# Both MLP up projections: the first four pairs' weights and pair 0's sums are made among the rows of the projection before, and the transposed quarters are asked for earlier

## The chip, the cores and the metric

One core of a Trainium2 chip runs the whole kernel. The metric is the time of one execution in microseconds (us) on the device; the kernel before takes 2149.13 us, the median of three runs (2148.42 to 2152.03).

The engines are called as in the profile: PE (TensorE, matmuls and transposes), DVE (VectorE), ACT (ScalarE), POOL (GpSimd) and SP (SyncE, which here only issues loads). Each runs its own queue of instructions in order, and semaphores tie the queues together.

## The reference, cut to what matters

A trunk of two layers runs over a sequence of 1024 rows and 1024 columns, all in float32. Each layer has a mixer (a gated short convolution in layer 0, latent attention in layer 1), whose output is projected, normed, gated and added to the stream, and then an MLP:

```
D_MODEL, SEQ, DEPTH, D_FF = 1024, 1024, 2, 4096

def squared_relu_mlp(h, w_up, w_down):
    return jnp.square(jax.nn.relu(h @ w_up)) @ w_down

# in each layer; y is the mixer's output (conv_out or attn_o projection)
x = x + g_m[:, None, :] * rmsnorm(y, norm_g[l, 1])
h = modulate(rmsnorm(x, norm_g[l, 2]), sh_f, sc_f)
y = squared_relu_mlp(h, mlp_up_w[l], mlp_down_w[l])
x = x + g_f[:, None, :] * rmsnorm(y, norm_g[l, 3])
```

The change touches the passage from the first of these lines to the start of `h @ w_up`. It comes twice: after conv_out in layer 0 (338 to 470 us of the profiled execution) and after attn_o in layer 1 (1457 to 1590 us).

## The kernel before, in words

**A product.** Every float32 operand is split into a high and a low part, and `mm` (L154 to L156) forms a product from three matmuls of 128x128 by 128x512. `split_w` (L158 to L160) makes the parts: ACT copies the high one (L159), DVE subtracts it for the low one (L160).

**The rows.** The projection ahead of the MLP (`down`) works in chunks of its contraction; in the last two chunks each of the eight tiles of 128 rows is one result `big` of two banks. In the middle chunk DVE adds it to the row's tile `y` (L870). In the last chunk a class `Seam` takes each row: DVE adds the result (L866) and multiplies by the gate (L328), ACT squares and sums (L271, L273), DVE forms the reciprocal (L278) and adds to the stream (L361), ACT squares again, and `flush` (L311) writes the normed row. The second half of row t is put down one row later, so that engines overlap. From row 5 on, `front` also transposes finished rows (PE, L409; ACT evacuates them with scale and shift, L410) and `back` splits the results (DVE, L420 and L421) one row later.

**The up projection** takes the columns of w_up in 16 pairs of two tiles of 128. A pair is a 2x2 block product by Winograd's scheme: 7 products instead of 8, each 4 steps of k by 3 matmuls, 84 matmuls in all. The right operands are made once: "11" and "21" from the first 512 rows (k tiles 0 to 7, `front0` and `back0`), and "22", "t1", "t2", "t3", "t4" from both halves in four quarters (`front1`, `back1`): in each quarter ACT evacuates two transposes, DVE makes four differences (L441, L443, L446, L448) and four low parts (L434) plus one more, nine DVE instructions in all, and ACT makes five high parts (L431). The left operands of a pair are made by `pair_sums`: DVE adds and subtracts blocks of two weight tiles (L510, L511, L515, L518), and the sums are split (t2, s2 and t3: names `uplo`, `s`). The tiles of one pair's products are `first` ("11"), then "21", t2 with s2 (key 6), t3 with "t3" (key 7), t2 with "t1" (5), t3 with "22" (3) and t2 with "t4" (4).

**The first pairs.** `first_pairs` bridges the time until the second half of the rows is normed. The pairs 0 to 3 need only "11" and "21" for their first two products, so these are run first, out of three weight tiles that were split ahead of the last chunk, and a fourth (`late`, name `w`) that comes in a buffer of its own. Pair 0's other five products are then run quarter by quarter as the quarters appear (`for kk in range(4)`). The order on PE, DVE and ACT is pinned there as it is written. Pairs 1 to 15 run in `all_pairs`: product 6, product 7, product 5, then 3 and 4, with `take` (L564) between 6 and 5 and between 5 and 3, since these three share one bank. The outputs of a pair are squared on ACT (L1150 to L1154), summed on DVE (L1161 to L1164) and stored by DMAs that ACT issues (L1166). A scheduler sets the order on each engine outside the pinned parts.

**Buffers.** `raw` tiles (512 KB) have four buffers for everything: weights, stream rows and the quarters' transposes. The split weights (`uphi`, `uplo`) have three each. The quarters' sums share one buffer (`gmb`).

## Time and profile before

| what | value |
|---|---|
| median of three runs | 2149.13 us (2148.42 to 2152.03) |
| the profiled execution | 2148.73 us, its span 2146.9 us |
| PE busy | 2057.8 us, 96% |
| DVE busy | 1542.4 us, 72% |
| ACT busy | 1085.8 us, 51% |
| mean granted TensorE clock | 0.992 |
| PE waits on other engines, 330 to 480 us | 10.4 us in 8 waits |
| the same in layer 1, 1455 to 1600 us | 10.6 us |

The span runs from the first to the last instruction, and 1.8 us of the profiled execution lie around it. A row of a timeline gives the start and the duration of an instruction (or of a few alike), then the engine, the line, what is written and read, and in square brackets the idle time before it with the engine and tile that ended it. A row of the waits gives the waiting instruction, what it waited for, the sum, the count and the longest. In the windows, PEclk is the clock that TensorE was granted, 1.00 being full speed.

### The profile page before, as it was taken

To read this page: it belongs to the slowest core of one execution; us is meant where nothing else is said; L and a number is where in the kernel's file an instruction comes from. 1 tells how busy PE (TensorE), PEld (TensorE's weight loads), DVE (VectorE), ACT (ScalarE), POOL (GpSimd) and SP (SyncE) were. 2 spreads that over 40 slices of the span, in tenths; PEclk is the share of its full clock that TensorE was granted. 3 is DMA by queue.
4 is the path that set the end of the run, shared out by engine and by line. 5 is a ranking of instruction groups with operands and counts; after the bars stand their busy time and mean duration, and the time that the engine had idled before them with its cause. 6 is when DMAs were issued, how large, how long until landed. Compare 5 with 4: busy or idle time off the path is not lost.

```text
span 2146.9 us, 25090 instructions
## 1 busy us (share of the span) xinstructions
PE 2057.8 (96%) x9438; PEld 1685.5 (79%) x9438; DVE 1542.4 (72%) x2100; ACT 1085.8 (51%) x1545; POOL 5.3 (0%) x13
## 2 busy tenths in 40 slices
PE   4999999899999999999899999999899999999998
PEld 3788878778888788888677788878678888788886
DVE  6877876875765669977688887757875665566577
ACT  4533354744554444455665565555644444544443
POOL 0000000000000000000000000000000000000000
PEclk9999999999999999999999999999999999999999
DMA  7444464254653889656223331144254653774255
GB/s 226 118 140 147 137 201 143 89 181 162 196 182 127 288 280 324 210 172 201 79 70 120 94 91 35 60 130 147 89 183 148 211 182 135 266 251 161 94 174 174
DMA packets 251167, 344.47 MB, mean 160 GB/s; under 512 B 19269, under 2 KB 142498, under 8 KB 251046
## 3 DMA queue, kind: packets, MB, share of 16 engines
q1 hardware_dynamic: 208840, 253.81, 37.7%
q10 hardware_dynamic: 42206, 89.06, 11.1%
q8 instruction: 74, 1.21, 0.2%
q14 instruction: 47, 0.39, 0.1%
HBM read 258.94 MB, written 83.89 MB: 160 GB/s over the span
## 4 chain that ended last, share of the span: by engine, by line
PE 74%; DVE 12%; ACT 6%; DMA 5%; issue 2%; SPq 0%; ACTq 0%; DVEq 0%
PE one L156 39%; PE mm L156 19%; PE tp L156 6%; PE big L156 5%; PE big L1397 2%; DMA raw<-ha 2%; DVE ring L160 1%; PE tp L1423 1%; ACT junk L271 1%; ACT slot L1247 1%; DMA w<-in_mlp_down_w_dram 1%; ACT ring L159 1%; DMA aw<-in_ada_w_dram 1%; DVE acc L186 1%; DVE uplo L160 1%
## 5 line engine op out<-in xcount | busy, mean ns | idle before, releaser
L156 PE MATMUL one<-slot,uphi 128*128 128x512 f32 x1224 | 377.9, 390 | 0.0
L156 PEld LDWEIGHTS one<-slot,uphi 128*128 128x128 f32 x1224 | 230.4, 188 | 48.2 <-issue 0.5
L156 PE MATMUL one<-ring,ring 128*128 128x512 f32 x1152 | 262.9, 389 | 2.3 <-DVE ring L160 2.3
L160 DVE TENSOR_TENSOR uplo<-raw,uphi 128x1024 fp32r<-128x1024 f32 x127 | 153.2, 1222 | 146.2 <-ACT uphi L159 146.2
L156 PEld LDWEIGHTS one<-ring,ring 128*128 128x128 f32 x1152 | 215.8, 188 | 48.3 <-ACT ring L159 3.1
L156 PE MATMUL one<-slot,uplo 128*128 128x512 f32 x612 | 240.7, 393 | 8.2 <-DVE y L564 3.8
L160 DVE TENSOR_TENSOR ring<-raw,ring 128x1024 fp32r<-128x1024 f32 x144 | 174.3, 1219 | 55.1 <-ACT ring L159 54.7
L159 ACT ACTIVATE ring<-raw 128x1024 fp32r<-128x1024 f32 x144 | 149.4, 1051 | 116.0 <-DMA raw<-ha 73.5
L159 ACT ACTIVATE uphi<-raw 128x1024 fp32r<-128x1024 f32 x127 | 134.6, 1061 | 122.0 <-PE one L156 80.2
L156 PE MATMUL mm<-ring,ring 128*128 128x512 f32 x768 | 185.0, 390 | 1.1 <-DVE ring L160 1.0
L156 PE MATMUL tp<-ring,ring 128*128 128x512 f32 x768 | 184.0, 389 | 0.0
L156 PEld LDWEIGHTS mm<-ring,ring 128*128 128x128 f32 x768 | 143.7, 188 | 31.7 <-DVE ring L160 1.4
L156 PEld LDWEIGHTS tp<-ring,ring 128*128 128x128 f32 x768 | 144.1, 188 | 29.9
L159 ACT ACTIVATE ring<-w 128x1024 fp32r<-128x1024 f32 x80 | 84.6, 1058 | 160.2 <-PE tp L156 86.6
L160 DVE TENSOR_TENSOR ring<-w,ring 128x1024 fp32r<-128x1024 f32 x80 | 97.7, 1221 | 77.5 <-ACT ring L159 76.8
L156 PEld LDWEIGHTS one<-slot,uplo 128*128 128x128 f32 x612 | 115.2, 188 | 35.9 <-DVE y L564 5.5
L186 DVE SCALAR_TENSOR_TENSOR acc<-raw,csil,acc 128x1024 f32<-128x1024 f32 x88 | 112.4, 1277 | 23.1 <-DMA raw<-in_ada_w_dram 18.3
L562 ACT ACTIVATE y<-one 128x512 f32<-128x512 f32 x66 | 39.0, 591 | 160.4 <-PE one L156 113.8
L156 PE MATMUL mm<-slot,uphi 128*128 128x512 f32 x344 | 107.4, 394 | 9.3 <-DVE slot L434 9.3
L156 PE MATMUL one<-slot,s 128*128 128x512 f32 x468 | 112.9, 390 | 1.1 <-DVE s L160 1.1
L156 PEld LDWEIGHTS one<-slot,s 128*128 128x128 f32 x468 | 87.6, 188 | 20.6 <-DVE s L160 2.4
L156 PE MATMUL one<-q,uphi 128*128 128x512 f32 x328 | 101.9, 392 | 0.0
(273 smaller groups left out, 3611.6 us busy)
## 6 DMA issues: line engine op xcount, KB each, us to landing
ha<-y ACTq DMA_DIRECT2D x224, 256.0 KB, 4.0
raw<-ha SPq DMA_DIRECT2D x112, 512.0 KB, 4.1
raw<-in_ada_w_dram SPq DMA_DIRECT2D x80, 512.0 KB, 4.2
raw<-in_mlp_up_w_dram SPq DMA_DIRECT2D x70, 512.0 KB, 4.5
w<-in_mlp_down_w_dram SPq DMA_DIRECT2D x48, 512.0 KB, 7.2
raw<-in_mlp_down_w_dram SPq DMA_DIRECT2D x32, 512.0 KB, 4.2
xs<-raw ACTq DMA_DIRECT2D x19, 512.0 KB, 3.1
raw<-in_conv_in_w_dram SPq DMA_DIRECT2D x18, 512.0 KB, 4.0
```

Of the source, the lines that this page charges most:

```text
L156: nc.tensor.matmul(out_, lhs[a], rhs[b], start=first and i == 0, stop=last and i == 2, skip_group_check=more)
L159: nc.scalar.activation(hi, src, AF.Copy)
L160: nc.vector.tensor_tensor(lo, src, hi.bitcast(F32), op=ALU.subtract)
L186: nc.vector.scalar_tensor_tensor(acc, raw, s, acc, op0=ALU.mult, op1=ALU.add)
L271: nc.scalar.activation(junk[:, :src.shape[-1]], src, AF.Square, accum_out=ss)
L562: nc.scalar.activation(dst, x_, AF.Copy)
L1247: nc.scalar.activation(y[32 * i:32 * i + 32, :], p_[32 * j:32 * j + 32, :], AF.Copy, scale=scale)
L1397: nc.tensor.matmul(o_, a, m_, start=j == 0, stop=j == 4)
L1423: nc.tensor.transpose(p_[:, c:c + P], pts[4 * hf + i][:, j * P:(j + 1) * P], ident)
```

## The change

In neutral words, and with the lines of the kernel after in brackets where they are meant:

1. The `ahead` step before the last chunk now splits four weight tiles instead of three, loads pair 0's two weight tiles and makes pair 0's sums and two of its three splits. `uphi` and `uplo` have five buffers each while the up stage lasts. The fourth weight tile takes a `raw` buffer; the buffer `late` is gone. The six loads stand on SP ahead of the rows' loads; three of them (two of pair 0, and `w`) stood behind them.
2. `Seam.tile` issues the transposes before the squares and the flush of the row, from row 5 on.
3. `first_pairs` runs first(0) and first(1) back to back, the four last "11"/"21" transposes behind them, and asks for each quarter's transposes one quarter earlier (`middle`, called in the midst of `back1`). The evacuations (`keep`, `gate`) are separate steps. Pair 0's products run in the order 3, 7, 5, 6, 4 in each quarter, 7 later in the last. t3's split stands behind quarter 0.
4. Pair 1's weights are loaded in `first_pairs`, and its sums are made there, behind the last quarter, by `pair_sums_apart`, which writes one difference into another tile. The last four of pair 0's additions (`finish`) and its store are handed to `all_pairs` and run in pair 1. Pair 1's result of product 7 goes to an `mm` bank.

The number of instructions of each engine is the same before and after, and so is what is computed. PE's order differs only in the passages named; DVE's, ACT's and SP's also differ through the rest of the up stage, since the scheduler has two more buffers of split weights there.

Three places in the order of DVE carry the prediction; all are in layer 0, and layer 1 has the like. First, the last rows of the middle chunk, before (L870 is a row's addition, L866 the last chunk's row 0):

```order
L160 TENSOR_TENSOR uplo_2605<-raw_2602,uphi_2604 128x1024
L870 TENSOR_TENSOR y_2272<-y_2272,big_2502 128x1024
L870 TENSOR_TENSOR y_2273<-y_2273,big_2516 128x1024
L870 TENSOR_TENSOR y_2274<-y_2274,big_2530 128x1024
L870 TENSOR_TENSOR y_2275<-y_2275,big_2544 128x1024
L866 TENSOR_TENSOR y_2268<-y_2268,big_2608 128x1024
```

and after, where L932 and L928 are the same additions, L525 to L533 pair 0's sums, and `uplo` and `s` the low parts of the splits:

```order
L172 TENSOR_TENSOR uplo_2611<-raw_2608,uphi_2610 128x1024
L525 TENSOR_TENSOR raw_2614<-raw_2614,raw_2616 128x512
L932 TENSOR_TENSOR y_2273<-y_2273,big_2516 128x1024
L526 TENSOR_TENSOR raw_2616<-raw_2616 128x512
L932 TENSOR_TENSOR y_2274<-y_2274,big_2530 128x1024
L172 TENSOR_TENSOR uplo_2621<-raw_2616,uphi_2620 128x1024
L530 TENSOR_TENSOR raw_2616<-raw_2616,raw_2614 128x512
L932 TENSOR_TENSOR y_2275<-y_2275,big_2544 128x1024
L172 TENSOR_TENSOR s_439_2626<-raw_2616,s_438_2625 128x512
L533 TENSOR_TENSOR raw_2614<-raw_2614,raw_2616 128x512
L928 TENSOR_TENSOR y_2268<-y_2268,big_2630 128x1024
```

Six instructions of pair 0 and the fourth weight's low part (`uplo_2611`) now stand between the rows' additions. Second, what stands ahead of the first quarter's first difference (L441), before:

```order
L420 CAST slot_2261<-q_2282 128x512
L421 TENSOR_TENSOR slot_2261<-q_2282,slot_2261 128x512
L278 RECIPROCAL small_3089<-small_3022 128x1
L160 TENSOR_TENSOR uplo_3106<-w_3041,uphi_3105 128x1024
L510 TENSOR_TENSOR raw_3043<-raw_3043,raw_3045 128x512
L511 TENSOR_TENSOR raw_3045<-raw_3045 128x512
L160 TENSOR_TENSOR uplo_3125<-raw_3045,uphi_3124 128x1024
L515 TENSOR_TENSOR raw_3045<-raw_3045,raw_3043 128x512
L160 TENSOR_TENSOR s_547_3143<-raw_3045,s_546_3142 128x512
L518 TENSOR_TENSOR raw_3043<-raw_3043,raw_3045 128x512
L441 TENSOR_TENSOR sums_3173<-raw_3128 128x512
```

and after (L453 is that difference):

```order
L432 CAST slot_2261<-q_2280 128x512
L433 TENSOR_TENSOR slot_2261<-q_2280,slot_2261 128x512
L290 RECIPROCAL small_3083<-small_3044 128x1
L432 CAST slot_2261<-q_2281 128x512
L433 TENSOR_TENSOR slot_2261<-q_2281,slot_2261 128x512
L432 CAST slot_2261<-q_2282 128x512
L433 TENSOR_TENSOR slot_2261<-q_2282,slot_2261 128x512
L453 TENSOR_TENSOR sums_3145<-raw_3118 128x512
```

The weight and the sums are gone from there, and the reciprocal (L278, now L290) on which the last row's flush waits stands four instructions earlier. Third, from the second `take` of pair 1 (L564) to the low part of pair 2's s2 (`s_592`), before:

```order
L564 TENSOR_TENSOR y_3403<-y_3038,one_3386 128x512
L1162 TENSOR_TENSOR y_3037<-y_3037,y_3371 128x512
L575 TENSOR_TENSOR y_3403<-y_3403,one_3430 128x512
L1163 TENSOR_TENSOR y_3417<-y_3037 128x512
L160 TENSOR_TENSOR uplo_3465<-raw_3459,uphi_3464 128x1024
L1164 TENSOR_TENSOR y_3418<-y_3371,y_3417 128x512
L515 TENSOR_TENSOR raw_3459<-raw_3459,raw_3457 128x512
L584 TENSOR_TENSOR y_3038<-y_3038,one_3386 128x512
L518 TENSOR_TENSOR raw_3457<-raw_3457,raw_3459 128x512
L160 TENSOR_TENSOR s_592_3470<-raw_3459,s_591_3469 128x512
```

and after, from the second instruction behind that `take` (now L604) on, L526 of pair 2 being the first:

```order
L615 TENSOR_TENSOR y_3346<-y_3346,mm_3430 128x512
L525 TENSOR_TENSOR raw_3562<-raw_3562,raw_3564 128x512
L526 TENSOR_TENSOR raw_3564<-raw_3564 128x512
L1234 TENSOR_TENSOR y_3098<-y_3098,y_3345 128x512
L172 TENSOR_TENSOR uplo_3465<-raw_3459,uphi_3464 128x1024
L1235 TENSOR_TENSOR y_3417<-y_3098 128x512
L530 TENSOR_TENSOR raw_3459<-raw_3459,raw_3457 128x512
L1236 TENSOR_TENSOR y_3418<-y_3345,y_3417 128x512
L533 TENSOR_TENSOR raw_3457<-raw_3457,raw_3459 128x512
L624 TENSOR_TENSOR y_3100<-y_3100,one_3395 128x512
L630 TENSOR_TENSOR y_3346<-y_3346,mm_3430 128x512
L172 TENSOR_TENSOR s_592_3470<-raw_3459,s_591_3469 128x512
```

Between the `take` and `s_592` stand now twelve instructions where there were eight: L525 and L526 of pair 3, L526 of pair 2 and L630, pair 1's last addition, have come into this stretch.

The diff, with the code that left `first_pairs` cut (it is printed above):

```
@@ -340,13 +352,13 @@
                     gained(slice(0, HALF if part else D))
                 else:
                     self.back()
+                if t >= 5:
+                    self.front(steps, 2)
                 if part:
                     ss = squares(self.nx, y[:, :HALF], some)
                 else:
                     ss = squares(self.nx, y)
                 self.flush()
-                if t >= 5:
-                    self.front(steps, 2)
                 rs = rroot(ss)
                 if not beside:
                     nc.vector.scalar_tensor_tensor(y, y, rs, self.gmb, op0=ALU.mult, op1=ALU.mult)
@@ -443,6 +455,7 @@
             part1("t1", kk, a)
             part2("22", kk, b)
+            middle()
             nc.vector.tensor_tensor(b, b, a, op=ALU.subtract)
             part1("t2", kk, b)
@@ -478,6 +491,8 @@
+    up_bufs = [3]
@@ -490,8 +505,8 @@
     def up_split(up, r3, kk=KD):
-        hi = up.tile([P, KD, P], F32R, tag="uphi", name=nm("uphi"), bufs=3)
-        lo = up.tile([P, KD, P], F32R, tag="uplo", name=nm("uplo"), bufs=3)
+        hi = up.tile([P, KD, P], F32R, tag="uphi", name=nm("uphi"), bufs=up_bufs[0])
+        lo = up.tile([P, KD, P], F32R, tag="uplo", name=nm("uplo"), bufs=up_bufs[0])
@@ -520,6 +535,22 @@
         t3 = up_split(up, a)
         yield {7: (t3, 0, "t3"), 3: (t3, 4, "22")}
+    def pair_sums_apart(up, a, b, s_):
+        a11, a12, a21, a22 = a[:, 0:4, :], a[:, 4:8, :], b[:, 0:4, :], b[:, 4:8, :]
+        s_ = s_.rearrange("p (k m) -> p k m", k=4)
+        nc.vector.tensor_tensor(a11, a11, a21, op=ALU.subtract)
+        nc.vector.tensor_tensor(s_, a22, a11, op=ALU.subtract)
+        s2 = tuple(up.tile([P, 4, P], F32R, tag="s2" + "hl"[i], name=nm("s2"), bufs=1) for i in range(2))
+        nc.scalar.activation(s2[0], s_, AF.Copy)
+        nc.vector.tensor_tensor(a21, a21, a22, op=ALU.add)
+        nc.vector.tensor_tensor(a12, a12, s_, op=ALU.subtract)
+        nc.vector.tensor_tensor(s2[1], s_, s2[0].bitcast(F32), op=ALU.subtract)
+        t3 = up_split(up, a)
+        yield {6: (s2, 0, "t2"), 7: (t3, 0, "t3"), 3: (t3, 4, "22")}
+        t2 = up_split(up, b)
+        yield {5: (t2, 0, "t1"), 4: (t2, 4, "t4")}
@@ -528,15 +559,18 @@
-    def all_pairs(up, ops, jobs):
...
-        end = []
+    def all_pairs(up, ops, jobs, end=()):
...
+        end, mark = list(end), None
         for raws, begun, quarter, done, between in jobs:
-            ra, rb = raws()
+            begun, *made = begun if isinstance(begun, tuple) else (begun,)
+            mark, mark_ = last_dve() if made else None, mark
+            if not made:
+                ra, rb = raws()
@@ -551,10 +585,16 @@
-            rest = {}
-            for part in pair_sums(up, ra, rb):
-                rest.update(part or {})
-            b = row_tile()
+            if made:
+                b, rest = made
+            else:
+                rest = {}
+                sums_ = pair_sums(up, ra, rb)
+                with behind(mark_):
+                    next(sums_)
+                for part in sums_:
+                    rest.update(part or {})
+                b = row_tile()
@@ -568,7 +608,7 @@
-            v = bank_ps()
+            v = mm_ps() if made else bank_ps()
             prod(v, rest[7], ops)
@@ -622,64 +662,86 @@
             seam.back()
         return ps_
...
+    def first_pairs(seam, steps0, steps1, up, wmat, ws, ops, pair):
         banks(True)
         tiles = [mm_ps(), mm_ps(), bank_ps(), bank_ps()]
...
+        ca = []
+        sums, rest = pair
         def first(i):
             prod(tiles[i], (ws[i], 0, "11"), ops)
+        def keep(i):
+            ca.append(row_tile())
             nc.scalar.activation(ca[i][:, HALF:], tiles[i], AF.Copy)
         def second(i):
             prod(tiles[i], (ws[i], 4, "21"), ops, False)
+        def gate(i):
             nc.scalar.activation(ca[i][:, :HALF], tiles[i], AF.Relu)
...
+        def front():
+            seam.front(steps1, 1)
+        def quarter(middle=lambda: None):
+            seam.backs.pop(0)(middle)
+        out_ = {}
+        def rest_of(kk, order):
+            for j in order:
+                prod(out_[j], rest[j], ops, kks=[kk])
         with pinned():
             first(0)
+            first(1)
+            seam.flush()
+            seam.front(steps0, 2)
+            keep(0)
+            keep(1)
+            first(2)
             seam.back()
...
+            front()
+            keep(2)
             second(0)
...
+            quarter(front)
+            gate(0)
+            rest.update(next(sums))
             second(1)
...
+            gate(1)
+            quarter(front)
             second(2)
...
+            gate(2)
             first(3)
...
+            keep(3)
+            out_.update({6: mm_ps(), 5: mm_ps(), 3: bank_ps(), 7: bank_ps(), 4: bank_ps()})
+            rest_of(0, (3, 7, 5, 6, 4))
+            quarter(front)
+            a, b = load_pair(wmat, 1)
+            second(3)
+            gate(3)
+            rest_of(1, (3, 7, 5, 6, 4))
+            quarter()
+            cb, b1 = row_tile(), row_tile()
+            rest_of(2, (3, 7, 5, 6, 4))
+            rest_of(3, (3, 5, 6, 7, 4))
+            sums = pair_sums_apart(up, a, b, b1[:, :HALF])
+            rest1 = next(sums)
+            p1 = ca[0][:, HALF:]
             c21, c22 = halves(cb)
             nc.vector.tensor_tensor(c21, p1, out_[6], op=ALU.add)
             nc.vector.tensor_tensor(c22, c21, out_[5], op=ALU.add)
+            rest1.update(next(sums))
+        def finish():
             nc.vector.tensor_tensor(c21, c21, out_[4], op=ALU.add)
             nc.vector.tensor_tensor(p1, c22, out_[3], op=ALU.add)
             nc.vector.tensor_tensor(c22, c22, out_[7], op=ALU.add)
             nc.vector.tensor_tensor(c21, c21, out_[7], op=ALU.add)
...
+        return ca, cb, (b1, rest1), finish
     def release_arena():
         for q in (ar[2], ar[1], ar[0]):
@@ -1132,13 +1194,23 @@
         steps0, steps1 = quarter_steps(ys, key, hs)
-        wcols = [next_w[:, 2 * i * P:(2 * i + 1) * P] for i in range(AHEAD - 1)]
-        down(slots, sizes, wd, src_fn, ys, seam, steps0, 0, lambda: ws.extend(up_weights(up, [w]) for w in wcols), begun)
-        return up, hs, first_pairs(seam, steps0, steps1, up, next_w, ws, hs)
+        wcols = [next_w[:, 2 * i * P:(2 * i + 1) * P] for i in range(AHEAD)]
+        up_bufs[0] = AHEAD + 1
+        pair = []
+        def ahead():
+            ws.extend(up_weights(up, [w]) for w in wcols)
+            sums = pair_sums(up, *load_pair(next_w, 0))
+            next(sums)
+            next(sums)
+            pair.extend([sums, next(sums)])
+        down(slots, sizes, wd, src_fn, ys, seam, steps0, 0, ahead, begun)
+        return up, hs, first_pairs(seam, steps0, steps1, up, next_w, ws, hs, pair)
     def mlp_up(l, up, ops, firsts, per_pair_bg):
-        ca, cb = firsts
+        ca, cb, made, finish = firsts
         late = []
         n = D_FF // P // 2
@@ -1174,14 +1246,16 @@
-        store(0, ca[0], cb)
-        end = all_pairs(up, ops, [(lambda i=i: load_pair(mlp_up_w[l], i), ca[i] if i < AHEAD else None, quarter,
-                                   lambda a, b, i=i: store(i, a, b), lambda i=i: between(i)) for i in range(1, n)])
+        begun = [None, (ca[1], *made), *ca[2:]] + [None] * (n - AHEAD)
+        end = all_pairs(up, ops, [(lambda i=i: load_pair(mlp_up_w[l], i), begun[i], quarter,
+                                   lambda a, b, i=i: store(i, a, b), lambda i=i: between(i)) for i in range(1, n)],
+                        [lambda: store(0, ca[0], cb), finish])
...
         up.release()
+        up_bufs[0] = 3
```

More of the change, by code (lines that the diff above doesn't have):

```diff
@@ L111, in pinned, with last_dve, behind @@
             last[ins.engine] = ins.name
+    def last_dve():
+        return [ins.name for ins in nc.cur_bb.bb.instructions if ins.engine == mybir.EngineType.DVE][-1]
+    @contextmanager
+    def behind(name):
+        n = len(nc.cur_bb.bb.instructions)
+        yield
+        if name:
+            ins = next(i for i in nc.cur_bb.bb.instructions[n:] if i.engine == mybir.EngineType.DVE)
+            tc.add_manual_dep(ins, name, NO_SYNC, reason="behind")
     def ld(out_, in_):
@@ L644, in first_pairs @@
             seam.back()
-            seam.front(steps0, 2)
-            first(1)
-            seam.back()
-            seam.flush()
+            front()
+            keep(2)
             second(0)
-            ws.append(up_split(up, late))
-            sums = pair_sums(up, a, b)
-            next(sums)
+            quarter(front)
+            gate(0)
+            rest.update(next(sums))
             second(1)
-            next(sums)
-            seam.front(steps1, 1)
-            rest = next(sums)
@@ L657, in first_pairs @@
-            first(2)
-            seam.front(steps1, 1)
-            seam.backs.pop(0)()
+            gate(1)
+            quarter(front)
             second(2)
-            rest.update(next(sums))
+            gate(2)
             first(3)
-            seam.front(steps1, 1)
-            seam.backs.pop(0)()
-            out_ = {6: mm_ps(), 5: mm_ps(), 3: bank_ps(), 7: bank_ps(), 4: bank_ps()}
-            for kk in range(4):
-                for j in (5, 6, 4, 3, 7):
-                    prod(out_[j], rest[j], ops, kks=[kk])
-                if kk == 0:
-                    second(3)
-                    seam.front(steps1, 1)
-                if kk < 2:
-                    seam.backs.pop(0)()
```

11 lines of the change are left out of this document (2 added, 9 removed).

## The prediction

> **What bounds the kernel now.** I read the page's busy times first, then PE's waits by stage, and last the timelines of PE, DVE and ACT in the stage that the change touches.
>
> ```profile
> PE 2057.8 (96%) x9438; PEld 1685.5 (79%) x9438; DVE 1542.4 (72%) x2100; ACT 1085.8 (51%) x1545; POOL 5.3 (0%) x13
> ```
>
> PE is busy for 96% of the span, so a change that adds and removes no work can only give back PE's waits, or make new ones. Here are PE's waits on other engines between 330 and 480 us, all of layer 0's passage:
>
> ```profile
> PE mm L156 <- DVE slot L434: 4.6, 2, 3.2
> PE one L156 <- DVE y L564: 1.9, 2, 1.1
> PE tp L409 <- ACT q L410: 1.4, 1, 1.4
> PE mm L156 <- ACT slot L431: 1.2, 1, 1.2
> PE one L156 <- ACT y L635: 1.1, 1, 1.1
> PE one L156 <- DVE s L160: 0.2, 1, 0.2
> ```
>
> They sum to 10.4 us. On PE's timeline the passage runs from row 6 of the last chunk to pair 3; the longest wait stands in it, and its twin of layer 1 in the second fence:
>
> ```profile
> 371.49 1.62 PE L156 MATMUL big<-slot 128*128 128x512 f32 x6
> ...
> 383.40 1.03 PE L409 MATMUL tp<-cs,y 128*128 128x128 f32 x8
> 384.19 0.48 PE L156 MATMUL mm<-slot,uplo 128*128 128x512 f32 x1
> ...
> 430.93 1.22 PE L156 MATMUL mm<-slot,uphi 128*128 128x512 f32 x2 [3.25 <-DVE slot L434]
> ...
> 436.31 2.90 PE L156 MATMUL one<-slot,s 128*128 128x512 f32 x12
> ...
> 451.38 3.02 PE L156 MATMUL one<-slot,s 128*128 128x512 f32 x12 [0.21 <-DVE s L160]
> ...
> 469.28 0.40 PE L156 MATMUL one<-slot,uplo 128*128 128x512 f32 x1
> ```
> ```profile
> 1550.41 1.22 PE L156 MATMUL mm<-slot,uphi 128*128 128x512 f32 x2 [3.24 <-DVE slot L434]
> ```
>
> 436.31 is the first product of pair 1, 451.38 that of pair 2, and 469.28 that of pair 3, so the passage from 371.49 takes 97.8 us. I work the sum out on layer 0 and take it twice. The windows beside the longest wait show a further cost:
>
> ```profile
> core 0: us, PE busy (x) PEld busy (x) DVE busy (x) ACT busy (x) POOL busy (x), PEclk, DMA share, GB/s
> 425.16:428.58 3.42, 1.35 (x5) 0.56 (x3) 3.42 (x6) 2.05 (x4) 0.00 (x0) 1.00 0.39 116
> 428.58:431.99 3.41, 1.06 (x3) 0.88 (x4) 3.41 (x6) 1.18 (x2) 0.00 (x0) 0.50 0.00 0
> 431.99:435.40 3.41, 3.41 (x10) 2.67 (x9) 2.62 (x5) 1.29 (x2) 0.00 (x0) 0.50 0.76 235
> 435.40:438.82 3.42, 3.42 (x16) 2.80 (x15) 2.44 (x4) 0.93 (x2) 0.00 (x0) 1.00 0.80 245
> ```
>
> From 428.58 to 435.40 the granted clock is half, so the full window 431.99 to 435.40 holds 10 matmuls where the next holds 16. DVE, in turn, is busy without a gap in the first two: it is what PE waits for.
>
> **The change part by part.** *DVE's chain.* These rows hold its start and end before:
>
> ```profile
> 397.00 1.23 DVE L160 TENSOR_TENSOR uplo<-w,uphi 128x1024 fp32r<-128x1024 f32 x1 [2.75 <-ACT uphi L159]
> ...
> 404.54 0.69 DVE L441 TENSOR_TENSOR sums<-raw 128x512 f32<-128x512 f32 x1
> ...
> 410.33 1.22 DVE L160 TENSOR_TENSOR uplo<-raw,uphi 128x1024 fp32r<-128x1024 f32 x1
> 411.46 0.69 DVE L441 TENSOR_TENSOR sums<-raw 128x512 f32<-128x512 f32 x1
> ...
> 417.37 0.69 DVE L441 TENSOR_TENSOR sums<-raw 128x512 f32<-128x512 f32 x1
> ```
>
> A quarter's nine instructions take 5.8 to 5.9 us (404.54 to 410.33, 411.46 to 417.37), t3's split 1.13 us. Four quarters and the split are 24.6 us. Ahead of the first, the weight and pair 0's sums held DVE from 397.00 to 404.54; they leave. What sets the start then is ACT, which must evacuate the first quarter's transposes:
>
> ```profile
> 391.96 0.43 DVE L420 CAST slot<-q 128x512 fp32r<-128x512 f32 x1 [1.17 <-ACT q L410]
> ...
> 394.09 0.16 DVE L278 RECIPROCAL small<-small 128x1 f32<-128x1 f32 x1
> ```
> ```profile
> 390.66 0.60 ACT L635 ACTIVATE y<-mm 128x512 f32<-128x512 f32 x1
> 391.15 1.45 ACT L410 ACTIVATE q<-tp,v,v 128x512 f32<-128x512 f32 x2
> ...
> 394.28 1.15 ACT L311 ACTIVATE y<-raw,small 128x1024 f32<-128x1024 f32 x1 [0.99 <-DVE small L278]
> ```
>
> The last row's flush waited for a reciprocal that stood behind eight casts and subtractions; it now stands behind four, so it can run at 390.8, where DVE had 1.17 us free. The flush then takes 391.0 to 392.1, two evacuations (1.45 for two in the row 391.15) to 393.5, two `keep` of 0.49 (390.66 to 391.15) to 394.5, and the first quarter's two evacuations to 395.9. DVE begins at about 396.0, 8.5 us earlier than 404.54, and ends the fourth quarter at 396.0 + 24.6 = 420.6. Pair 1's sums follow: four subtractions or additions and s2's low part at 0.6 to 0.7 each are 3.5 us, so pair 1's first product may start at 424.2.
>
> PE has 204 matmuls and 56 transposes from 371.49 to that product. At 0.227 us a matmul (twelve from 436.31 to 439.06, in rows above and below, are 2.75 with a turn of 0.03) and 0.099 a transpose (eight from 383.40 to 384.19) this is 51.8 us, and about 0.6 for turns between the two kinds; PE is there at 423.9. The wait is 0.3. The quarters themselves come in time: a quarter's fifteen matmuls take 3.4 us, so PE starts the third's at 423.9 − 6.8 = 417.1, and DVE has it at 396.0 + 18.7 = 414.7; the fourth's last product starts at 423.2, and DVE is done at 420.6. Five of the eight waits go, and the half clock with them. At pair 1's first product the gain is 436.31 − 424.2 = 12.1 us.
>
> *The moved cover.* The weight and pair 0's sums are now among the middle chunk's rows and cost DVE 5.9 us there (two of 1.23 as at 397.00, five of 0.69 as at 404.54). The rows of layer 0 and then of layer 1 at that place:
>
> ```profile
> 338.25 1.22 DVE L870 TENSOR_TENSOR y<-y,big 128x1024 f32<-128x1024 f32 x1 [1.50 <-PE big L156]
> 343.69 1.22 DVE L866 TENSOR_TENSOR y<-y,big 128x1024 f32<-128x1024 f32 x1 [4.22 <-PE big L156]
> ```
> ```profile
> 1453.38 2.35 DVE L870 TENSOR_TENSOR y<-y,big 128x1024 f32<-128x1024 f32 x2
> 1457.73 1.22 DVE L870 TENSOR_TENSOR y<-y,big 128x1024 f32<-128x1024 f32 x1 [2.00 <-PE big L156]
> 1463.17 1.22 DVE L866 TENSOR_TENSOR y<-y,big 128x1024 f32<-128x1024 f32 x1 [4.22 <-PE big L156]
> ```
>
> Layer 0 has three gaps of 1.50 and one of 4.22: free. Layer 1 has 2.00 and 4.22, 6.2 for 5.9: also free, with row 0 perhaps a microsecond late, which PE would feel only when it comes back to that result's banks two rows later. I take 0, and 1 us as its upper bound. Of the six loads, three move ahead of the stream rows on SP; those rows are wanted several microseconds later, so I take 0.
>
> *What is given back.* From pair 1's second `take` to pair 2's s2 the order shows twelve instructions where eight stood. Before:
>
> ```profile
> 439.06 0.39 PE L156 MATMUL one<-slot,uplo 128*128 128x512 f32 x1
> ...
> 445.44 0.50 PE L156 MATMUL one<-slot,uplo 128*128 128x512 f32 x1 [0.78 <-DVE y L564]
> ```
> ```profile
> 444.69 0.69 DVE L564 TENSOR_TENSOR y<-y,one 128x512 f32<-128x512 f32 x1 [0.55 <-PE one L156]
> ...
> 450.64 0.68 DVE L160 TENSOR_TENSOR s<-raw,s 128x512 fp32r<-128x512 f32 x1
> ```
>
> The eight and the `take` filled 5.95 us without a gap (eight at 0.60 and a split at 1.13), and PE, ready 0.21 earlier, started pair 2 at 451.38. Four more at 0.6 are 2.4 us: a wait of 0.2 becomes one of 2.6, and pair 2 starts at 424.2 + (451.38 − 436.31) + 2.4 = 441.7 instead of 451.38. The gain left is 9.7 us. From there to 469.28 the same work follows in the same order on PE, with the wait of 1.13 kept.
>
> *The clock.* A wait of 2.6 us may cost half speed again. Before, a window in which PE was busy for 1.35 of 3.42 us (40%) was followed by one at 0.50. If the wait falls mostly into one such window, which about 7 of 10 phases give (1.9 of it must), the next is at half clock: 3.41 / 2 = 1.7 us.
>
> *The sum.* Two places at 9.7 are 19.4 us, less 2 × 0.7 × 1.7 = 2.4 for the clock: 17.0. From the profiled execution's 2148.73 us (0.4 under the median of 2149.13) this gives 2131.7; with half clock at both places 2132.7 (19.4 less twice 1.7).
>
> **The rivals.** *The clock holds*: only a window without any work drops it, and no wait of 2.6 us fills one of 3.4. Then nothing comes off the 19.4 us: 2129.3. Against it stands the window of 40% that was followed by one at 0.50; for it, that this window was followed by another, of 31%, so that one alone isn't shown to do it. The Trainium skill, "TensorE: Matmul & The Clock Gate", Part 1, "What's actually happening", gives this rule: half rate comes after at least one idle window of about 3.4 us.
>
> *No give-back*: DVE's queue at pair 2 is loose enough that the four additions run in the gaps before the `take` (0.55 in the row 444.69). For it speaks that L525 needs only a load; against it that the order puts them behind. Then 12.1 a place, 2124.5.
>
> *DVE's chain starts late*: ACT's queue before the first quarter, or a transposed row, holds it 4 us longer; the 2.75 us that DVE waited for ACT ahead of 397.00 show that ACT's queue can. Pair 1 waits for DVE already, so each microsecond late is lost there. Gain 5.7 a place, less 3.4 for clock: 2140.7.
>
> *The change doesn't reach its point*: the first quarter starts at 404.5 as before, since the rows and not the sums set it. Fourth quarter at 429.1, pair 1 at 432.7, gain 3.6 less 2.4: 1.2 a place, 2146.3. The 2.75 us of idle ahead of 397.00 and the flush's start at 394.28 speak for a part of it.
>
> *Slower*: the scheduler's new order in the later pairs. If s2 comes late in each of the 14 later pairs of each layer as it does in pair 2, 28 waits of 2.6 us are 73 us: 2204.5. It decides from 0.76 us a pair on (17.0 + 4.3 over 28).
>
> ```profile
> 545.50:621.50 76.00, 76.00 (x337) 62.94 (x336) 53.41 (x69) 38.46 (x49) 0.00 (x0) 1.00 0.66 206
> ```
>
> Against it: in this window of four pairs PE never stops and DVE is busy for 53 of 76 us, so each pair has 5 us to spare; five buffers let s2 be made a pair ahead.
>
> **How the numbers follow.** Forecast 0.52, the clock holds 0.12, no give-back 0.08, late chain 0.16, point missed 0.07, slower 0.05. A measurement of this kernel tells 0.2%, 4.3 us, from no change: the first four are faster (0.88), the fifth within (0.07), the last slower (0.05). The range 2124 to 2142 holds the forecast, with layer 1's bound of 1 us, the two cases above it and the late chain up to 4 us; outside lie the last two and a chain later still, near 2 in 10.
>
> **What would show it.** Right: the waits on L434 (after: L446) of 1.4 and 3.25 are gone, the first quarter starts 8 us earlier, pair 1 starts 12 us earlier counted from row 6, and a new wait of 2 to 3 us stands at pair 2's s product. Wrong: the first quarter starts within 3 us of where it did, a wait above 0.5 us recurs in the later pairs, or PE waits in the middle chunk of layer 1 for longer than 1 us.

## The result, and the profile after

The changed kernel takes 2133.11 us (median of four runs, 2131.19 to 2133.8); the kernel before took 2149.64 in the same comparison (2148.42 to 2152.03). The ratio is 0.992, with a 95% interval of 0.9908 to 0.9931: faster by 16.5 us. The forecast was 2131.7. The profiled execution has a span of 2131.0 us, 15.9 less than before.

PE's waits on other engines between 330 and 480 us, in the kernel after (L604 is `take`, L172 a split's low part):

```profile
PE one L168 <- DVE s L172: 2.7, 1, 2.7
PE one L168 <- DVE y L604: 1.6, 2, 0.8
```

Six rows have become two: the two waits on L434, those on L410, L431 and L635 are gone, the one on `s` has grown from 0.2 to 2.7. Between 1440 and 1600 us, in layer 1, the same two rows stand, and the wait of 0.4 in its middle chunk is gone as well. Their places on PE's timeline, layer 0 first:

```profile
372.51 1.62 PE L168 MATMUL big<-slot 128*128 128x512 f32 x6
...
425.35 3.02 PE L168 MATMUL one<-slot,s 128*128 128x512 f32 x12
434.58 0.50 PE L168 MATMUL one<-slot,uplo 128*128 128x512 f32 x1 [0.78 <-DVE y L604]
...
443.05 3.02 PE L168 MATMUL one<-slot,s 128*128 128x512 f32 x12 [2.73 <-DVE s L172]
...
452.29 0.50 PE L168 MATMUL one<-slot,uplo 128*128 128x512 f32 x1 [0.78 <-DVE y L604]
...
460.58 0.39 PE L168 MATMUL one<-slot,uplo 128*128 128x512 f32 x1
```
```profile
1483.14 0.71 PE L421 MATMUL tp<-cs,y 128*128 128x128 f32 x5
...
1536.09 3.04 PE L168 MATMUL one<-slot,s 128*128 128x512 f32 x12
...
1553.81 4.61 PE L168 MATMUL one<-slot,s 128*128 128x512 f32 x12 [2.73 <-DVE s L172]
...
1572.96 0.39 PE L168 MATMUL one<-slot,uplo 128*128 128x512 f32 x1
```

The row that the prediction calls pair 3's first product (469.28 before, 460.58 here) is its second: its s product has been run among pair 2's last products (462.92 before, 457.18 here). From pair 2's first product to that row both kernels run the same 72 matmuls, so it serves as the end of the passage all the same, and "to pair 3" below means this row. From row 6 (372.51) to it (460.58) the passage takes 88.1 us instead of 97.8. In layer 1, measured from the transposes in row 6 (1483.14, before 1491.68) to 1572.96 (before 1588.81), it takes 89.8 instead of 97.1. The two differences, 9.7 and 7.3 us, sum to 17.0. The span moved by 15.9: of the other 1.1 us, 0.8 is a wait of PE at the start of conv_out (1.0 us before, 1.8 after), ahead of any instruction that was moved, on a weight that landed later. The same kernel run again waits 1.4 us there, so this part differs from one execution to the next.

The layers differ in one thing. Twelve matmuls of pair 2's s product take 3.02 us in layer 0 and 4.61 in layer 1. The windows around the wait, layer 0 and then layer 1 (after the width: PE, PEld, DVE, ACT, POOL, then PEclk, DMA share and GB/s):

```profile
437.90:441.31 3.41, 2.43 (x11) 1.69 (x9) 3.41 (x6) 0.31 (x1) 0.00 (x0) 1.00 0.41 154
441.31:444.73 3.42, 1.68 (x7) 1.42 (x8) 2.82 (x4) 3.42 (x5) 0.00 (x0) 1.00 0.28 97
444.73:448.14 3.41, 3.41 (x16) 2.82 (x16) 1.98 (x3) 1.22 (x2) 0.00 (x0) 1.00 1.08 294
```
```profile
1550.65:1554.06 3.41, 0.68 (x3) 0.25 (x3) 3.41 (x7) 2.30 (x3) 0.00 (x0) 1.00 0.41 154
1554.06:1557.47 3.41, 3.41 (x9) 2.63 (x9) 0.83 (x1) 2.64 (x4) 0.00 (x0) 0.50 0.70 185
1557.47:1560.89 3.42, 3.42 (x16) 2.80 (x16) 2.36 (x4) 0.00 (x0) 0.00 (x0) 1.00 1.05 344
```

The same wait of 2.73 us is split over two windows in layer 0 (PE busy for 71% and 49% of them) and the clock holds; in layer 1 it lies in one (20%), and the next window is at half clock, with 9 matmuls instead of 16.

DVE's side of it in layer 0, with the first quarter's first difference (L453), t3's split behind that quarter, the low part of pair 1's s2 (L548), and the second `take` and the s2 of pair 2:

```profile
396.52 0.69 DVE L453 TENSOR_TENSOR sums<-raw 128x512 f32<-128x512 f32 x1 [0.76 <-ACT raw L422]
...
402.53 1.23 DVE L172 TENSOR_TENSOR uplo<-raw,uphi 128x1024 fp32r<-128x1024 f32 x1
...
424.60 0.69 DVE L548 TENSOR_TENSOR s<-y,s 128x512 fp32r<-128x512 f32 x1 [0.63 <-ACT s L545]
...
433.84 0.69 DVE L604 TENSOR_TENSOR y<-y,one 128x512 f32<-128x512 f32 x1 [0.34 <-PE one L168]
...
442.32 0.68 DVE L172 TENSOR_TENSOR s<-raw,s 128x512 fp32r<-128x512 f32 x1
```

The first quarter starts 24.0 us behind row 6 (before 33.1). From the `take` to s2 DVE runs 8.48 us without a gap (before 5.95).

### The profile page after: what moved, and what is told of

Same layout as the page of the kernel before. It is cut to its first block, busy times and chain, and to the rows that moved or that the text cites. A ratio compares the mean times of both kernels' runs of the same rounds, so it can differ in the third digit from the quotient of the medians.

```text
span 2131.0 us, 25054 instructions
## 1 busy us (share of the span) xinstructions
PE 2054.8 (96%) x9438; PEld 1686.4 (79%) x9438; DVE 1553.8 (73%) x2100; ACT 1082.5 (51%) x1545; POOL 5.6 (0%) x13
## 3 DMA queue, kind: packets, MB, share of 16 engines
q10 hardware_dynamic: 42206, 89.06, 11.2%
## 4 chain that ended last, share of the span: by engine, by line
PE 78%; DVE 10%; ACT 5%; DMA 4%; issue 2%; SPq 0%; ACTq 0%; DVEq 0%
PE one L168 40%; PE mm L168 20%; PE big L168 7%; PE tp L168 6%; PE big L1471 2%; DMA raw<-ha 2%; DVE ring L172 1%; PE tp L1497 1%; ACT slot L1321 1%; DVE acc L198 1%; ACT junk L283 1%; ACT ring L171 1%; PE tp L421 1%; DVE raw L373 0%; DMA raw<-in_ada_w_dram 0%
## 5 line engine op out<-in xcount | busy, mean ns | idle before, releaser
L168 PE MATMUL one<-slot,uphi 128*128 128x512 f32 x1208 | 372.1, 389 | 0.0
L172 DVE TENSOR_TENSOR uplo<-raw,uphi 128x1024 fp32r<-128x1024 f32 x129 | 157.6, 1222 | 85.5 <-ACT uphi L171 85.3
L172 DVE TENSOR_TENSOR ring<-raw,ring 128x1024 fp32r<-128x1024 f32 x144 | 174.2, 1219 | 59.0 <-ACT ring L171 58.6
L172 DVE TENSOR_TENSOR ring<-w,ring 128x1024 fp32r<-128x1024 f32 x80 | 97.6, 1220 | 74.1 <-ACT ring L171 73.1
L168 PE MATMUL one<-q,uphi 128*128 128x512 f32 x312 | 96.0, 389 | 0.0
L168 PE MATMUL big<-slot,slot 128*128 128x512 f32 x384 | 93.8, 391 | 1.8 <-ACT y L930 1.8
```

Source lines behind the costliest of these rows:

```text
L168: nc.tensor.matmul(out_, lhs[a], rhs[b], start=first and i == 0, stop=last and i == 2, skip_group_check=more)
L172: nc.vector.tensor_tensor(lo, src, hi.bitcast(F32), op=ALU.subtract)
```

## The experiments

The theory: pair 1 can start when DVE has worked through four quarters and pair 1's sums, so what counts is how early DVE's chain begins and what stands in it; what the change pushed behind pair 1 comes back as the wait at pair 2. The rivals: the rows or ACT set the start whatever DVE does, and the wait at pair 2 is a load's or PE's. All runs in one table, the passages from row 6 in the profiled execution of each, layer 0 / layer 1:

| kernel | to pair 1, us | to pair 3, us | median, us |
|---|---|---|---|
| before | 64.8 / 64.2 | 97.8 / 97.1 | 2149.6 |
| changed | 52.8 / 53.0 | 88.1 / 89.8 | 2133.1 |
| changed, run again | 52.8 / 52.9 | 88.1 / 89.7 | 2132.7 |
| sums back (1) | 57.6 / 58.3 | 94.4 / 95.1 | 2143.7 |
| first edit alone (2) | 62.9 / 63.4 | 95.8 / 96.4 | 2158.9 |
| evacuations ahead of the quarter (3) | 55.6 / 55.6 | 92.5 / 92.5 | 2140.8 |
| second edit undone (4) | 53.5 / 52.8 | 90.3 / 89.6 | 2135.9 |
| pair 1 as before (5) | 54.2 / 54.4 | 90.4 / 90.4 | 2134.6 |
| wait filled (6) | 52.8 / 52.8 | 88.1 / 88.1 | 2131.1 |
| pair 0's sums one pair later (7) | 52.8 / 52.8 | 86.3 / 86.7 | 2128.2 |
| three pairs' sums one pair later (8) | 52.8 / 53.0 | 85.5 / 86.1 | 2125.9 |

The kernel before measured 2149.9, 2152.0 and 2149.9 us beside the later groups of runs, so medians of different groups carry 1 or 2 us.

**1. Pair 0's sums back in their place.**

```
         def ahead():
             ws.extend(up_weights(up, [w]) for w in wcols)
-            sums = pair_sums(up, *load_pair(next_w, 0))
-            next(sums)
-            next(sums)
-            pair.extend([sums, next(sums)])
...
-        sums, rest = pair
+        a, b = load_pair(wmat, 0)
...
             front()
             keep(2)
+            sums = pair_sums(up, a, b)
+            next(sums)
+            next(sums)
+            rest = next(sums)
             second(0)
```

> The changed kernel with pair 0's sums and two splits put back where they were, between the casts of the last transposes and the first quarter; the fourth weight stays among the middle chunk's rows. Theory (DVE's chain sets when pair 1 starts): five instructions of 0.6 to 0.7 us and a split, with two waits for ACT's high parts, push the first quarter from 396.5 to about 401.9 us, and the 5.4 us are lost one for one at both places: about 2144 us, pair 2's wait of 2.7 us unchanged. Rival (the rows and ACT's evacuations set the start, the sums stood in idle time): the first quarter moves by less than 1 us, 2133 to 2135 us.

Measured: 2143.66 us (ratio to before 0.997, 0.996 to 0.998). DVE's timeline of this run:

```profile
395.88 0.69 DVE L525 TENSOR_TENSOR raw<-raw,raw 128x512 f32<-128x512 f32 x1
396.60 0.69 DVE L526 TENSOR_TENSOR raw<-raw 128x512 f32<-128x512 f32 x1
398.42 1.22 DVE L172 TENSOR_TENSOR uplo<-raw,uphi 128x1024 fp32r<-128x1024 f32 x1 [1.13 <-ACT uphi L171]
399.68 0.69 DVE L530 TENSOR_TENSOR raw<-raw,raw 128x512 f32<-128x512 f32 x1
401.07 0.69 DVE L172 TENSOR_TENSOR s<-raw,s 128x512 fp32r<-128x512 f32 x1 [0.70 <-ACT s L171]
401.68 0.69 DVE L533 TENSOR_TENSOR raw<-raw,raw 128x512 f32<-128x512 f32 x1
402.28 0.68 DVE L453 TENSOR_TENSOR sums<-raw 128x512 f32<-128x512 f32 x1
```

Six instructions and two waits for ACT stand ahead of L453, which starts 29.6 us behind row 6, 5.6 later than in the changed kernel. Pair 1 starts 4.8 and 5.3 us later; the rest of the time lost is the clock, at half for one window behind the wait at pair 2 in both layers, and in layer 1 also behind a wait of 3.5 us for an evacuation of ACT's (window 1523.27 to 1526.69). The sums' place alone is worth 10 of the 16 us, if the other edits are there. With the sums in their old place the rest of the change still starts pair 1 earlier than before, by 7.2 and 5.9 us.

**2. The first edit alone**, put into the kernel before: the `ahead` step and the five buffers of the diff, and in `first_pairs` only the lines that made the weight and the sums taken out:

```
-        a, b = load_pair(wmat, 0)
         with pinned():
...
             second(0)
-            ws.append(up_split(up, late))
-            sums = pair_sums(up, a, b)
-            next(sums)
             second(1)
-            next(sums)
             seam.front(steps1, 1)
-            rest = next(sums)
             first(2)
```

> The kernel before with the first edit alone: four weights and pair 0's sums among the middle chunk's rows, five buffers; the order of the first pairs, the transposes and pair 1 as before. Theory: the first quarter can start only when ACT has evacuated its transposes, which PE makes behind second(1), so at about 400.2 instead of 404.5 us; the three waits inside pair 0's quarters and the half clock go, pair 1 starts about 6 us earlier a place, and no new wait comes at pair 2: 2136 to 2140 us, so some 10 of the 16 us. Rival A (the sums alone made the wait): all of the gain, 2132 us or lower. Rival B (without the earlier transposes the sums' place is worth nothing): 2146 us or more.

Measured: 2158.85 us, slower than before (ratio 1.0042, 1.0027 to 1.0057). The expectation failed twice. In the passages only 2.0 and 0.7 us were gained. DVE begins 4.4 us earlier behind row 6, as expected, and then stops after two instructions:

```profile
399.46 0.69 DVE L441 TENSOR_TENSOR sums<-raw 128x512 f32<-128x512 f32 x1 [5.86 <-ACT raw L410]
400.19 0.69 DVE L443 TENSOR_TENSOR raw<-raw,q 128x512 f32<-128x512 f32 x1
403.59 0.69 DVE L434 TENSOR_TENSOR slot<-raw,slot 128x512 fp32r<-128x512 f32 x1 [2.71 <-ACT slot L431]
```
```profile
401.10 0.60 ACT L636 ACTIVATE y<-one 128x512 f32<-128x512 f32 x1 [1.68 <-PE one L156]
401.60 1.44 ACT L410 ACTIVATE raw<-tp,v,v 128x512 f32<-128x512 f32 x2
402.92 0.64 ACT L431 ACTIVATE slot<-raw 128x512 fp32r<-128x512 f32 x1
```

ACT's queue holds the quarter's first high part (L431) behind a copy that waits for PE and behind the next quarter's evacuations. I had counted DVE's instructions and ACT's evacuation of this quarter, but not what the old order puts between. The second loss lies outside the passages, at the start of each MLP down projection:

```profile
714.12 2.27 PE L156 MATMUL one<-ring,ring 128*128 128x512 f32 x4 [4.80 <-DVE ring L160]
```

Before and in the changed kernel PE waits 1.15 us there, 24 matmuls in; here it waits 4.80 at the first one, and half clock follows. That is about 6 us in each layer, which makes 12 less 2.7, the 9 us by which it is slower. The first down weight is loaded later. Its row in this run, and then in the changed kernel:

```profile
706.63 0.37 SPq L114 DMA_DIRECT2D w<-in_mlp_down_w_dram  x1
```
```profile
688.46 0.37 SPq L126 DMA_DIRECT2D w<-in_mlp_down_w_dram  x1
```

Counted from the last pair's second `take` (703.59 and 697.28 on PE) the load comes 3.0 us behind it here and 8.8 us ahead of it in the changed kernel. SP's waits between 650 and 716 us hold one of 19.9 us for PE here, so the load probably waits until PE has read a weight whose memory it overwrites. Both kernels have five buffers; why the place differs between the two wasn't tried, and the cause stays open.

**3. The evacuations ahead of the quarter**, in the changed kernel:

```
             second(0)
-            quarter(front)
+            front()
+            quarter()
```

and so in the two other places of `quarter(front)`.

> The changed kernel with one part of the third edit undone: each quarter's transposes are evacuated by ACT ahead of the quarter before, as in the kernel before, and not in its midst. Theory (found in the run of the first edit alone, where DVE waited 2.71 us for ACT's first high part behind such an evacuation): the first quarter stalls 2 to 3 us in its midst, and pair 1 starts that much later: 2137 to 2140 us with the clock. Rival (that stall came from the older order of PE's products): within 1 us of the changed kernel.

Measured: 2140.81 us (ratio 0.9956, 0.9941 to 0.997), 8 us over the changed kernel beside it (2132.73). The quarter starts as it did and stops in the same place as in run 2:

```profile
395.85 0.69 DVE L453 TENSOR_TENSOR sums<-raw 128x512 f32<-128x512 f32 x1 [0.77 <-ACT raw L422]
396.57 0.69 DVE L455 TENSOR_TENSOR raw<-raw,q 128x512 f32<-128x512 f32 x1
399.90 0.69 DVE L446 TENSOR_TENSOR slot<-raw,slot 128x512 fp32r<-128x512 f32 x1 [2.63 <-ACT slot L443]
```

Pair 1 starts 2.7 and 2.6 us later at the two places, and both fall to half clock at pair 2, which layer 0 does not in the changed kernel. So ACT's order alone is worth 8 of the 16 us, with everything else in place. This overlaps with the 10 us of run 1: the quarters start early only if DVE and ACT are both free. That PE makes the transposes earlier was not tried alone.

**4. The second edit undone**: the transposes behind the flush in `Seam.tile`.

> The changed kernel with the second edit undone: the transposes of rows 5 to 7 stand behind the squares and the flush again. Theory: ACT comes to the last row's second squares about 0.7 us later, the first quarter starts 0.7 us later and pair 1 with it, one for one: 1 to 2 us in all over the changed kernel, 2134 to 2135. Rival A: this order carried much of the earlier start, 4 us a place, 2141 us. Rival B: nothing, within 0.7 us of the changed kernel.

Measured: 2135.91 us (2133.18 to 2139.59), beside 2132.73 for the changed kernel. To pair 1 layer 0 takes 0.65 us longer, as expected, layer 1 nothing; the passage of layer 0 has half clock at pair 2 where the changed kernel's has none (90.3 for 88.1). The profiled run is the longest of the five and has a further wait of 2.04 us at 840 us, in code that is the same in both. The size is small, and the run can't say more.

**5. Pair 1 as before**: its sums by `pair_sums` in the loop, pair 0's additions and store at once.

```
-            sums = pair_sums_apart(up, a, b, b1[:, :HALF])
-            rest1 = next(sums)
...
-            rest1.update(next(sums))
-
-        def finish():
...
-        begun = [None, (ca[1], *made), *ca[2:]] + [None] * (n - AHEAD)
+        store(0, ca[0], cb)
+        begun = [None, ca[1], *ca[2:]] + [None] * (n - AHEAD)
```

> The changed kernel with pair 1 treated as before: its sums by the old function inside the loop of pairs, pair 0's six additions and its store at once. Theory (the new wait at pair 2 comes from what was pushed behind pair 1): DVE has pair 1's sums between the fourth quarter's parts, so pair 1 starts 1 to 2 us later (near 427 us), but only eight instructions stand between the take and pair 2's s2, and the wait of 2.7 us is gone: pair 2 starts about 1.3 us earlier a place, and no window falls to half clock: 2128 to 2131 us. Rival (pair 1's early sums carry part of the gain): 2136 us or more.

Measured: 2134.55 us (ratio 0.9923, 0.9907 to 0.994), the same as the changed kernel within the spread; 2128 to 2131 was expected. Pair 1 starts 1.3 and 1.5 us later, as expected. The wait at pair 2 is gone too, but another has taken its place:

```profile
PE one L168 <- DVE y L604: 3.6, 2, 2.7
PE one L168 <- DVE s L172: 1.4, 1, 1.4
```
```profile
433.92 0.69 DVE L525 TENSOR_TENSOR raw<-raw,raw 128x512 f32<-128x512 f32 x1 [1.38 <-DMA raw<-in_mlp_up_w_dram]
434.53 0.69 DVE L1229 TENSOR_TENSOR y<-y 128x512 f32<-128x512 f32 x1
435.13 0.69 DVE L526 TENSOR_TENSOR raw<-raw 128x512 f32<-128x512 f32 x1
435.73 0.69 DVE L1230 TENSOR_TENSOR y<-y,y 128x512 f32<-128x512 f32 x1
436.33 0.68 DVE L604 TENSOR_TENSOR y<-y,one 128x512 f32<-128x512 f32 x1
```

Pair 1's second `take` (L604, 436.33) now stands behind pair 0's sums and behind an addition of pair 3 that waits for its load. The window behind the new wait is at half clock in both layers (436.97 to 440.38 and 1553.12 to 1556.54). The theory's account of the place was too narrow: the fourth edit neither makes nor saves DVE work in this stretch, it only chooses where PE meets it.

**6. The wait filled.** Twelve matmuls behind pair 1's last product, into a bank that is never read:

```
-            def fourth(v=v, rest=rest):
-                prod(v, rest[4], ops, False)
+            def fourth(v=v, rest=rest, made=made):
+                with pinned([mybir.EngineType.PE]):
+                    prod(v, rest[4], ops, False)
+                    if made:
+                        w_, k0_, n_ = rest[4]
+                        fill = tp_ps()
+                    for kk_ in range(4 if made else 0):
+                        mm(fill, (w_[0][:, k0_ + kk_, :], w_[1][:, k0_ + kk_, :]), ops[n_][kk_], kk_ == 0, kk_ == 3)
```

> The changed kernel with twelve further matmuls on PE between pair 1's last product and pair 2's first, into a bank that nobody reads: 2.7 us of PE work in the wait of 2.7 us, which stays as it is in DVE's queue. Theory (the half clock behind that wait comes from PE's share of work in the window, and costs 1.7 to 2 us where it falls): pair 2 starts when it did, within 0.3 us, and neither layer shows half clock there, so both passages from row 6 to pair 3 take 88 us; a run gains 0 to 3.4 us, some 2 us on the median: 2130 to 2132. Rival (the filling collides with DVE's or ACT's work on the banks, or the drop has another cause): pair 2 starts later, or a window behind the wait is still at half clock, 2133 or more.

Measured: 2131.06 us (2128.97 to 2132.33; ratio 0.9912, 0.9895 to 0.9928). Pair 2's first product in layer 0 and layer 1:

```profile
443.17 3.02 PE L168 MATMUL one<-slot,s 128*128 128x512 f32 x12
```
```profile
1553.63 3.01 PE L168 MATMUL one<-slot,s 128*128 128x512 f32 x12
```

Pair 2 starts 70.6 us behind row 6 in both layers, as in the changed kernel's layer 0 (443.05 less 372.51 is 70.5), and neither passage shows half clock: 88.1 and 88.1. So PE's idleness in that window is what drops the clock, as far as one profiled execution shows it, and the price of the half clock is the 1.7 us by which layer 1's passage is shorter than 89.8. The medians agree with that (2132.73 for the changed kernel, on another chip), but their ranges overlap.

**7. Pair 0's sums one pair later**, in the changed kernel:

```
         def between(i):
-            flush()
+            if i > 1:
+                flush()
```

> The changed kernel with the sums of pair 0's outputs (four DVE additions and seven stores) run one pair later. Theory (pair 2's wait is DVE's queue, 12 instructions behind the take): seven stand there now, s2 comes about 3 us earlier, the wait of 2.7 us falls to 0.3 or less at both places and layer 1 keeps its full clock: 2125 to 2128 us. Rival (the wait is PE's or a load's, DVE only happens to be last): the wait stays above 1.5 us and the time within 2 us of 2133.

Measured: 2128.21 us (2126.8 to 2132.21; ratio 0.9902, 0.9887 to 0.9917). Five instructions fewer stand between the `take` and s2, and the wait of 2.73 us is gone at both places. PE's wait at pair 2's own second `take` grows in return, from 0.78 us to 1.64 in layer 0 and 2.0 in layer 1. On DVE that `take` now stands right behind the last of pair 0's sums (L1236), which waits for a store:

```profile
440.91 3.01 PE L168 MATMUL one<-slot,s 128*128 128x512 f32 x12
451.01 0.50 PE L168 MATMUL one<-slot,uplo 128*128 128x512 f32 x1 [1.64 <-DVE y L604]
```
```profile
449.66 0.69 DVE L1236 TENSOR_TENSOR y<-y,y 128x512 f32<-128x512 f32 x1 [0.62 <-DMA ha<-y]
450.27 0.68 DVE L604 TENSOR_TENSOR y<-y,one 128x512 f32<-128x512 f32 x1
```

**8. Three pairs' sums one pair later each**, so that pairs 1 to 3 have no two of them:

```
         def between(i):
-            flush()
+            if i >= AHEAD:
+                flush()
+            elif i > 1:
+                late.pop(0)()
```

> The changed kernel with the sums of pairs 0 to 3 each run one pair later, so that no pair has two of them. Theory (DVE's queue in pairs 1 to 3 is all that PE waits for): as with pair 0's sums alone moved, pair 2's wait is gone, and the wait of 1.6 to 2.0 us at pair 2's second take, which that run showed in its place, falls to about 0.8: 2125 to 2127 us, 1 to 2 us under that run's 2128.2. Rival (result tiles held a pair longer run short and stall others): 2128 us or more.

Measured: 2125.9 us (2124.27 to 2126.78; ratio to before 0.9882, 0.9869 to 0.9896), beside 2132.73 for the changed kernel on the same chip. It is also 2.3 us under run 7, which ran on another chip. The expectation describes the edit wrongly: the sums of pairs 0, 1 and 2 run a pair later and those of pair 3 do not, so pair 4 has two (DVE's rows of L1233 at 476.34 and 479.24). It costs nothing there, since PE waits for no engine between 455 and 640 us. Layer 0's list of PE's waits has one row left:

```profile
PE one L168 <- DVE y L604: 1.6, 2, 0.8
```

The changed kernel was also run unaltered beside runs 3, 4 and 8:

> The changed kernel itself, unaltered, as the measure for the two runs beside it, on the same chip. All theories: 2131 to 2135 us, with a wait of 2.7 us at pair 2's s2 in both layers; which of the two places falls to half clock may differ from the first profile, since it depends on where the wait lies against the clock's windows.

Measured: 2132.73 us (2131.55 to 2133.95), with the same waits, and half clock again in layer 1 alone.

## Why the prediction was right, point by point

*The chain's start.* Forecast 24.5 us behind row 6 (396.0 less 371.49), measured 24.0. Runs 1 and 3 show that both halves of the reason are needed: DVE free of the sums, and ACT free of the next quarter's evacuations. The prediction priced the first and took the second for granted: it followed ACT up to the first quarter's evacuations and no further. In the kernel after that was enough; in run 2 the same omission gave an expectation that was wrong by about 20 us, together with a wait at another place.

*Pair 1.* Forecast gain 12.1 us, measured 12.0 (64.8 to 52.8) and 11.2 in layer 1. PE waits 0.09 us there instead of 0.3: DVE and PE meet, as worked out. Part of this is luck: DVE's chain began 0.5 us earlier than forecast, and a wait of 0.63 for ACT's high part of s2 (row 424.60), which the prediction's 3.5 us for pair 1's sums left out, used that up.

*The moved cover.* Taken at 0 with a bound of 1 us in layer 1; PE shows no wait in either middle chunk, and the 0.4 us of before is gone. In runs 1, 4, 7 and 8 PE waits 0.2 to 0.3 us there in layer 1, within the bound. Right.

*What is given back.* Twelve instructions for eight at 0.6 us: forecast a wait of 2.6, measured 2.73. Runs 7 and 8 confirm the cause: with five of them moved away the wait vanishes. Forecast gain at pair 2 was 9.7, measured 9.4 in layer 0.

*The two takes.* The wait of 1.13 us was to stay; it is 0.78. That is the 0.35 us by which the passage ended at 9.7 after all, though pair 2 had gained 0.3 us less: a small error of the sum, cancelled by another.

*The clock.* Forecast: 7 in 10 that such a wait drops it, 1.7 us each. Counting the changed kernel's two profiles and runs 1, 3 and 4, which all have the wait of 2.7 us at both places, 8 of 10 were followed by half clock, and run 6 gives 1.7 us. The ten are not independent: in both profiles of the changed kernel layer 0 keeps the clock and layer 1 loses it. The forecast's 7 in 10 was poorly founded: the 1.9 us that it asked of one window stands in none of its rows. Its own row, 1.35 us busy of 3.42, leaves 2.07 us of idle time, which a wait of 2.6 us gives in only 5 or 6 of 10 places. The rival that only an empty window drops the clock falls by the row 1550.65, where PE worked for 0.68 of 3.41 us. The rule of the Trainium skill, "TensorE: Matmul & The Clock Gate", Part 1, "What's actually happening" (half rate after at least one idle window of about 3.4 us), would have kept the clock there; the measurement decides. On the other side, 49% kept it at 441.31.

*The rivals.* The later pairs lost nothing: from pair 3 to the last third of the up stage PE runs as before. No stall came from the loads in layer 1. The late chain and the missed point didn't occur in this kernel; run 3 is what a chain held up by 2.7 us costs, 8 us in all with the clock, where the prediction put 9 for 4 us.

*The sum.* 17.0 us forecast, 17.0 in the passages, 16.5 in the medians. That the first two agree so well is luck: half clock fell on one place of two, 1.7 us instead of the 2.4 taken off, and layer 1, whose passage was 0.7 us shorter before, gained 0.7 less even without it (9.7 and 7.3 are 19.4 less 1.7 less 0.7).

## What to carry to other kernels

Where PE waits in several places along one chain of another engine, find the chain's first instruction and ask what each queue holds ahead of it and between its first instructions: taking work off DVE gained 2.7 us of these waits alone, and some 10 once the other edits, ACT's moved evacuations above all, were there too. Count the instructions between the event that releases the helper engine and the one that PE needs; here 0.6 us for each gave the new wait to 0.1 us, and moving work that nobody waits for (pair sums and stores) a pair later gave it back. A wait that filled most of a clock window cost half that window again (1.7 us), and the same wait spread over two windows cost nothing more; whether two short waits are always cheaper than one long one wasn't tried.

## What the runs showed of the hardware that was not expected

A window in which PE was busy for 20% (0.68 of 3.41 us) was followed by half clock for exactly one window, and one of 49% wasn't; an empty one isn't needed. The bounds of the stretches at half clock lie multiples of 3.413 us apart in each trace. Cut along these windows from 70 us on, the eleven profiles agree: all 38 windows at full clock in which PE was busy for 46% or less were followed by one at 0.50, none with more than 58% was, and in between both occurred. Moved weights can cost time far away: in run 2 the next stage's first load was issued 3.0 us behind the last pair's second `take`, where the changed kernel issues it 8.8 us ahead, and PE stood 4.80 us.
